# Four of eight experts on 64 slots, with both parts of the tokens side by side

## The chip, the core and the metric

The kernel runs on one core of a Trainium2 chip. A core has TensorE (PE in the profile; its weight loads are shown apart, as PEld), VectorE (DVE), ScalarE (ACT), GpSimd (POOL) and SyncE (SP), which have instruction queues of their own and wait for one another through semaphores. Here SP issues nearly all DMA transfers. The metric is the device time of one execution, in microseconds (us), as the median of several runs.

## What is computed

Two layers of a decoder trunk on 256 tokens of width 1024, in float32. Each layer is a mixer, a cross attention to 256 memory tokens and a feed-forward part. The feed-forward part is dense in the first layer and a mixture of eight experts in the second. Only the mixture matters here; its hidden width is 2816 (11 x 256).

```python
def swiglu(h, w_gate, w_up, w_down):
    a = jnp.einsum("bsd,df->bsf", h, w_gate)
    u = jnp.einsum("bsd,df->bsf", h, w_up)
    return jnp.einsum("bsf,fd->bsd", jax.nn.silu(a) * u, w_down)

def moe_swiglu(h, router_w, w_gate, w_up, w_down):
    logits = jnp.einsum("bsd,de->bse", h, router_w).astype(jnp.float32)
    top_v, top_i = lax.top_k(logits, TOP_K)          # TOP_K = 2, N_EXPERTS = 8
    top_w = jax.nn.softmax(top_v, axis=-1)
    gates = jnp.sum(jax.nn.one_hot(top_i, N_EXPERTS) * top_w[..., None], axis=-2)
    y = jnp.zeros(h.shape, jnp.float32)
    for e in range(N_EXPERTS):
        y = y + gates[..., e:e + 1] * swiglu(h, w_gate[e], w_up[e], w_down[e])
    return y
```

256 tokens choose two experts each, so the eight lists hold 512 entries, 64 on average. The reference's router, evaluated on the reference's inputs, gives the experts 0 to 7 lists of 61, 68, 51, 64, 63, 68, 68 and 69 tokens.

## The kernel before

**Products in three passes.** A float32 product is made of float32r products: both operands are split into a part `h` (high) and a rest `l` (low), and `mm3` (L325 to L328) adds low times high, high times low and high times high. So a tile of the weights passes through TensorE three times: its high part twice (L326 with the tokens' low part as stationary operand, L328 with their high part), its low part once (L327).

**Weights.** All weights come in tiles of [128, 2048] float32 (1 MiB, 1.049 MB). `weight_order` lists them in the order of their use. `load` (L134) issues a tile's DMA on SP into a free stage buffer; a buffer is free again when its tile has been split. In the mixture there are eleven stage buffers: four in the pool `wst`, four in `wst2` and three that `spare` takes elsewhere (`wsp` in the rows). `halve` splits a tile: for each half of 1024 columns ACT writes the high part `wh` (L143), then DVE writes the rest `wl` in two pieces of `CUT` = 512 columns (L147). The halves lie in rings of `HALVES` = 5 tiles [128, 1024] each for `wh` and `wl`, that is, two and a half weight tiles. `w` hands out the next tile and sees to it that the tiles up to two behind it (`split_ahead`) are split.

**The mixture (`moe`).** The router's choice is made on the chip: `route` gives `pos`, the place of each token in each expert's list (from 1; 0 where the expert isn't taken), and `pp`, whose last eight columns are the lengths of the lists. `prepare` and `gather` fetch the tokens of two experts at a time: one-hot matrices `oh` [tokens, 128 slots] times the tokens give each expert its 128 slots, feature-major (`xg`), again as a high and a low part. Every expert has 128 slots, whatever its list's length. An expert has 11 chunks (256 hidden columns each). A chunk takes two tiles `gu` (gate and up side by side, 2 x 4 blocks of 128 features) and one tile `dn`:

- `eg`: 8 blocks x 3 passes of 512 columns (24 matmuls) on the expert's tokens give [128 slots, gate 256 | up 256];
- `es`: ACT takes the silu of the gates (L1141), DVE multiplies it by the ups (L1142);
- `turn`: PE transposes `es` (2 transposes, L1087), ACT and DVE split the result into `ehh` and `ehl` (L336, L340);
- `down`: 2 x 2 x 3 = 12 matmuls add to `ed` [128 slots, 1024].

At an expert's end `evacuate` splits `ed` into `yh` and `yl`, and `scatter` brings the rows back to the tokens (`ez`, 8 matmuls) and adds them, times the gates, to the residual stream `x` (L1128). These steps overlap: the transposes belong to the chunk before, `down` to the one before that. Each engine's instructions run in the order in which the Tile scheduler placed them.

The experts run in the order 0 to 7. Behind the last one a register holds the longest list's length (`longest`); where it is over 128, a loop goes over all eight experts again for the slots from 128 on.

**Where it stands in time.** In the profile the mixer, the cross attention and the dense part of both layers take the first 580 us, the router 580 to 598 us, and the eight experts 598 to 1390 us.

Of the kernel before, what the change touches and what calls it, by code (L numbers as in the profile page):

```python
# [7 lines left out]
F32 = mybir.dt.float32  # L8
# [8 lines left out]
P = 128  # L17
# [40 lines left out]
class Halves:  # L58
    """A weight tile [128, 2048] as two tiles of its columns, each freed on its own."""
# [10 lines left out]
class Trunk:  # L70
    """The whole network as one Tile program; the residual stream stays in SBUF.

    A float32 product is three passes of float32r: both operands are split exactly into a
    part of float32r's precision and the rest, and only rest * rest (below float32's last
    bit) is left out.
    """

    def __init__(self, ctx, tc, a, out):
# [5 lines left out]
        self.split_ahead = 1  # L84
        self.build()

# [1 line left out]
    def weight_order(self):  # L88
# [3 lines left out]
        for l in range(DEPTH):  # L92
# [21 lines left out]
            else:  # L114
                m = l // 2
                gu = [(("gu", l, e * NFC + fc, k), a["moe_gu"][m, e, fc, k])
                      for e in range(E) for fc in range(NFC) for k in range(2)]
                dn = [(("dn", l, e * NFC + fc), rows(a["moe_w_down"][m, e], fc)) for e in range(E) for fc in range(NFC)]
# [9 lines left out]

    def load(self, src):
        """A weight tile into a free stage buffer."""  # L130
        slot = self.free.pop(0)
        st = slot()
        dst = st.rearrange("p (a b) -> p a b", b=src.shape[2]) if len(src.shape) == 3 else st
        self.fetched = self.nc.sync.dma_start(dst, src)  # L134
        return slot, st

    def halve(self, slot, st):
        """hi + lo = a staged tile; its buffer is free again."""
        nc, tc = self.nc, self.tc
        wh, wl = [Halves(*[self.wp.tile([P, 1024], F32R, name=n) for _ in range(2)]) for n in ("wh", "wl")]  # L140
        for q in range(2):
            s = slice(q * 1024, (q + 1) * 1024)
            self.halved = nc.scalar.activation(wh[:, s], st[:, s], AF.Copy)  # L143
            for c in range(0, 1024, CUT):
                s = slice(q * 1024 + c, q * 1024 + c + CUT)
# [5 lines left out]
    def spare(self):  # L151
        """One more stage buffer."""
# [19 lines left out]
    def w(self, *key):  # L172
        """The next weight tile, as two float32r parts [128, 2048]."""
# [6 lines left out]
    def build(self):  # L180
# [20 lines left out]
        with tc.tile_pool(name="mid", bufs=1) as self.md, tc.tile_pool(name="wkb", bufs=2) as self.wb:  # L201
            with tc.tile_pool(name="tmp", bufs=1) as tmp:
# [8 lines left out]
                # NEG where the column is beyond the row, and where it is before it  # L211
# [10 lines left out]
                # sel[p, h] is one where p is h or 32 + h  # L222
# [10 lines left out]
                # slot numbers along the row (from 1), and e' < e  # L233
# [31 lines left out]
        with tc.tile_pool(name="emid", bufs=1) as self.md, tc.tile_pool(name="ewkb", bufs=2) as self.wb, \  # L265
# [3 lines left out]
            self.xg = [self.big("xg", shape=(P, 2 * KD * P)) for _ in range(3)]  # L269
# [3 lines left out]
    def warm(self, n):  # L273
        """Keeps the tensor engine's clock up where it would wait."""
# [1066 lines left out]
```

## Time and profile before

| what | value |
|---|---|
| median of 3 runs | 1406.48 us (1405.11 to 1407.85) |
| the profiled execution, span from the first to the last instruction | 1404.0 us |
| PE busy | 1376.4 us (98%) |
| PEld busy | 1156.1 us (82%) |
| DVE busy | 1218.4 us (87%) |
| ACT busy | 946.2 us (67%) |
| moved by DMA | 368.09 MB, mean 262 GB/s |

The median is 2.5 us over the profiled execution's span; sums below are made against the span. The profile's page gives the busy time of each engine, then 40 equal slices of the span with the busy share of each engine in tenths, then the DMA queues, the chain of work that ended last, and the costliest groups of instructions. An instruction's duration runs from its start to the end of its last write, and the next one on the same engine may start before that end; so what an instruction costs its engine is the distance to the next start, and this is read from the timeline.

### The profile page before, as it was taken

The page shows a single profiled execution, that of the slowest core. Times are in us where ns is not written, and L with a number is a line of the kernel's source. Part 1 is how long each engine was busy: PE and PEld are TensorE (multiplying, and loading weights), DVE is VectorE, ACT ScalarE, POOL GpSimd, SP SyncE. Part 2 cuts the span into 40 slices and gives each one's busy share as a digit, 9 for nine tenths or more (in the row PEclk, how much of TensorE's full clock was granted, in tenths as well). Part 3 has the DMA queues.
Part 4 walks back from the last instruction along what each step waited for, and adds up shares of the span by engine and source line. Part 5 has one row for each costly group of instructions (what it writes and reads, how often), then busy time and mean ns, then how long its engine had stood idle before and what let it go on. Part 6 is the DMA issues. An engine that isn't in the chain of part 4 may idle for free.

```text
span 1404.0 us, 21087 instructions
## 1 busy us (share of the span) xinstructions
PE 1376.4 (98%) x7489; PEld 1156.1 (82%) x7489; DVE 1218.4 (87%) x2556; ACT 946.2 (67%) x1457; POOL 8.1 (1%) x30
## 2 busy tenths in 40 slices
PE   9999999999999999799999999999999999999996
PEld 9878989999998778688888888888788888888884
DVE  7988876655688887799999999899999999999997
ACT  7565575444455646587877877777777777777774
POOL 0000000000000000000000000000000000000000
PEclk9999999999999999899999999999999999999998
DMA  8422635555454224779988999889999989999870
GB/s 311 172 73 118 210 105 204 194 189 180 180 188 157 83 91 179 280 297 364 367 338 333 362 344 366 334 318 346 357 354 364 353 318 353 350 363 366 317 273 33
DMA packets 67569, 368.09 MB, mean 262 GB/s; under 512 B 5744, under 2 KB 6000, under 8 KB 38016
## 3 DMA queue, kind: packets, MB, share of 16 engines
q1 hardware_dynamic: 67136, 365.59, 69.7%
q8 instruction: 61, 1.00, 0.3%
q0 software_dynamic: 320, 1.08, 0.2%
q14 instruction: 52, 0.43, 0.1%
HBM read 365.60 MB, written 1.05 MB: 261 GB/s over the span
## 4 chain that ended last, share of the span: by engine, by line
PE 90%; DVE 5%; ACT 2%; DMA 2%; issue 1%; DVEq 0%; ACTq 0%; SPq 0%; POOL 0%; POOLq 0%
PE eg L327 11%; PE eg L326 11%; PE eg L328 11%; PE fm L327 6%; PE fm L326 6%; PE fm L328 6%; PE ed L326 5%; PE ed L328 5%; PE ed L327 5%; DVE wl L147 3%; PE tm L327 2%; PE tm L328 2%; PE tm L326 2%; PE pr L326 1%; PE pr L327 1%; PE pr L328 1%
## 5 line engine op out<-in xcount | busy, mean ns | idle before, releaser
L147 DVE TENSOR_TENSOR wl<-wst,wh 128x512 fp32r<-128x512 f32 x1100 | 694.6, 685 | 106.0 <-ACT wh L143 103.6
L143 ACT ACTIVATE wh<-wst 128x1024 fp32r<-128x1024 f32 x550 | 562.1, 1058 | 183.3 <-PE fm L328 90.9
L327 PE MATMUL eg<-wl,xg 128*128 128x512 f32 x704 | 282.4, 401 | 0.1
L326 PE MATMUL eg<-wh,xg 128*128 128x512 f32 x704 | 278.9, 396 | 0.0
L328 PE MATMUL eg<-wh,xg 128*128 128x512 f32 x704 | 278.1, 395 | 0.0
L326 PE MATMUL fm<-hTh,wl 128*128 128x256 f32 x736 | 206.8, 281 | 0.3 <-DVE wl L147 0.3
L327 PE MATMUL fm<-hTl,wh 128*128 128x256 f32 x736 | 206.2, 280 | 0.0
L328 PE MATMUL fm<-hTh,wh 128*128 128x256 f32 x736 | 205.6, 279 | 0.0
L147 DVE TENSOR_TENSOR wl<-wsp,wh 128x512 fp32r<-128x512 f32 x280 | 175.5, 686 | 11.0 <-ACT wh L143 10.0
L326 PEld LDWEIGHTS eg<-wh,xg 128*128 128x128 f32 x704 | 132.3, 188 | 31.0
L327 PEld LDWEIGHTS eg<-wl,xg 128*128 128x128 f32 x704 | 132.3, 188 | 30.2 <-DVE wl L147 1.2
L328 PEld LDWEIGHTS eg<-wh,xg 128*128 128x128 f32 x704 | 132.4, 188 | 29.4
L143 ACT ACTIVATE wh<-wsp 128x1024 fp32r<-128x1024 f32 x140 | 142.4, 1055 | 13.9 <-ACT wh L143 7.0
L326 PEld LDWEIGHTS fm<-hTh,wl 128*128 128x128 f32 x736 | 138.4, 188 | 1.1 <-DVE wl L147 0.4
L327 PE MATMUL ed<-wl,ehh 128*128 128x512 f32 x352 | 139.2, 395 | 0.0
L328 PE MATMUL ed<-wh,ehh 128*128 128x512 f32 x352 | 139.1, 395 | 0.0
L327 PEld LDWEIGHTS fm<-hTl,wh 128*128 128x128 f32 x736 | 138.4, 188 | 0.9 <-issue 0.2
L328 PEld LDWEIGHTS fm<-hTh,wh 128*128 128x128 f32 x736 | 138.4, 188 | 0.0
L326 PE MATMUL ed<-wh,ehl 128*128 128x512 f32 x352 | 133.4, 405 | 0.0
L1141 ACT ACTIVATE es<-eg,xr 128x256 f32<-128x256 f32 x88 | 41.9, 477 | 71.5 <-PE eg L328 71.5
L328 PEld LDWEIGHTS ed<-wh,ehh 128*128 128x128 f32 x352 | 66.0, 188 | 15.7
L327 PEld LDWEIGHTS ed<-wl,ehh 128*128 128x128 f32 x352 | 66.1, 188 | 14.2
(297 smaller groups left out, 1702.8 us busy)
## 6 DMA issues: line engine op xcount, KB each, us to landing
wst<-in_moe_gu_dram SPq DMA_DIRECT2D x130, 1024.0 KB, 5.0
wst<-in_moe_w_down_dram SPq DMA_DIRECT2D x64, 1024.0 KB, 5.0
wsp<-in_moe_gu_dram SPq DMA_DIRECT2D x46, 1024.0 KB, 5.0
wsp<-in_moe_w_down_dram SPq DMA_DIRECT2D x24, 1024.0 KB, 5.0
wst<-in_ffn_gu_dram SPq DMA_DIRECT2D x22, 1024.0 KB, 4.8
wst<-in_w_in_fm_dram SPq DMA_DIRECT2D x16, 1024.0 KB, 5.0
wst<-in_ffn_w_down_dram SPq DMA_DIRECT2D x11, 1024.0 KB, 4.8
wst<-in_w_in_tm_dram SPq DMA_DIRECT2D x8, 1024.0 KB, 5.0
```

Source lines behind the costliest of these rows:

```text
L143: self.halved = nc.scalar.activation(wh[:, s], st[:, s], AF.Copy)
L147: nc.vector.tensor_tensor(wl[:, s], st[:, s], wh[:, s].bitcast(F32), op=ALU.subtract)
L326: nc.tensor.matmul(out, ll, rh, start=start, stop=False)
L327: nc.tensor.matmul(out, lh, rl, start=False, stop=False)
L328: nc.tensor.matmul(out, lh, rh, start=False, stop=stop)
L1141: nc.scalar.activation(s, pg[:, 0:256], AF.Silu, scale=xr)
```

## The change

1. **Order of the experts.** `sort` (new, called in `moe` behind the gates) ranks the lists of experts 0 to 6 by length on DVE and writes the experts' numbers in that order to `ids`; SP loads these seven numbers into registers. Expert 7 stays first (place 0), since its weights are loaded before the router has run. The places 1, 3, 5 and 7 get the four shortest of the seven lists, the places 2, 4 and 6 the three longest. The weights of the places 1 to 7 are loaded from addresses that depend on these registers (`expert_gu`, `expert_dn`). `pos` and `gates` are brought into the same order.
2. **Short experts.** The places 1, 3, 5 and 7 run `short`: 64 slots. The stationary operand of a pass is [128 features, 64 slots high | 64 slots low], so each of `wl` and `wh` passes once; the rows 0 to 63 of the result belong to the high part, the rows 64 to 127 to the low one. ACT copies the result from PSUM (`eg`); `turn` is now four products of `eg` with `comb`, a [128, 64] matrix that adds both parts, times 1 / rms; then ACT's silu, DVE's product and the split. `ehh` holds both parts side by side too, and `down` has 8 matmuls for 12.
3. **Gather.** The groups are (0), (1, 2), (3, 4), (5, 6), (7) instead of pairs. A short list's one-hot columns are written twice, and its gather takes 64 columns.
4. **Splits of 1024 columns.** From the mixture on DVE writes `wl` in one piece for each half (`CUT[1]` = 1024).
5. **Buffers.** `wst2` has three buffers instead of four, `xg` two big tiles instead of three, and the freed tile is one more `spare`: again eleven stage buffers.
6. **The loop behind the end** runs where a list of the places 1, 3, 5, 7 is over 64, or another over 128; it then goes over all eight experts.

`evacuate` and `scatter` are moved out of `expert` with the same content. The core of the diff:

```diff
-CUT = 512
-STAGES = (4, 4)
+CUT = (512, 1024)
+STAGES = (4, 3)
+C = 64
+NSHORT = 4
+PLACES = (None, 0, 4, 1, 5, 2, 6, 3)
+GROUPS = ((0,), (1, 2), (3, 4), (5, 6), (7,))
...
+    def expert_gu(self, m, q, fc, hf):
+        gu = self.a["moe_gu"]
+        if q == 0:
+            return gu[m, E - 1, fc, hf]
+        return lambda: gu[m, bass.ds(self.ids[PLACES[q]], 1), fc, hf].rearrange("o p n -> p (o n)")
...
-            for c in range(0, 1024, CUT):
-                s = slice(q * 1024 + c, q * 1024 + c + CUT)
+            for c in range(0, 1024, self.cut):
+                s = slice(q * 1024 + c, q * 1024 + c + self.cut)
...
-            self.xg = [self.big("xg", shape=(P, 2 * KD * P)) for _ in range(3)]
+            self.xg = [self.big("xg", shape=(P, 2 * KD * P)) for _ in range(2)]
+            self.spare()
...
+    def sort(self, pos, gates, pp):
+        nc, md = self.nc, self.md
+        F = E - 1
+        cnt = md.tile([P, E], F32, name="cnt")
+        nc.vector.tensor_copy(cnt, pp[:, 2 * E:3 * E])
...
+        nc.vector.tensor_tensor(g2, oth, own, op=ALU.is_equal)
+        nc.vector.tensor_tensor(g1, oth, own, op=ALU.is_lt)
...
+        nc.vector.tensor_scalar(ids, num[:, 0], -1.0, None, op0=ALU.add)
...
+        self.ids = [nc.values_load(ids[0:1, r:r + 1], engines=[mybir.EngineType.SP], min_val=0, max_val=F - 1)
+                    for r in range(F)]
...
+        def short(gu, dn, x, xr, oh, gate, at):
...
+            both = x.rearrange("p k s t -> p k (s t)")
+            comb = wb.tile([P, C], F32, name="comb")
+            nc.vector.tensor_scalar(comb, eye, xr, None, op0=ALU.mult)
+            def turn(fc, g):
+                pt = self.psum((P, 4, C), "et")
+                for b in range(4):
+                    nc.tensor.matmul(pt[:, b, :], g[:, b * P:(b + 1) * P], comb, start=True, stop=True)
+                s = wb.tile([P, 256], F32, name="es")[:, 0:2 * C].rearrange("p (k t) -> p k t", t=C)
+                nc.scalar.activation(s, pt[:, 0:2, :], AF.Silu)
+                nc.vector.tensor_tensor(s, s, pt[:, 2:4, :], op=ALU.mult)
+                h = wb.tile([P, 2, P], F32R, name="ehh", bufs=3).rearrange("p k (s t) -> p k s t", t=C)
+                self.split(h[:, :, 0, :], h[:, :, 1, :], s)
+                later(lambda: down(fc, h))
+            def down(fc, h):
+                wh, wl = dn(fc)
+                for n in range(2):
+                    for k in range(2):
+                        fs = slice(k * 1024 + n * 512, k * 1024 + (n + 1) * 512)
+                        for w in (wl, wh):
+                            nc.tensor.matmul(ps[n], h[:, k].rearrange("p s t -> p (s t)"), w[:, fs], start=fc == 0 and k == 0 and w is wl,
...
+                        for w in (wl, wh):
+                            nc.tensor.matmul(pg, both[:, c], w[:, fs], start=c == 0 and w is wl,
+                                             stop=c == KD - 1 and w is wh)
+                g = wb.tile([P, 512], F32, name="eg", bufs=1)
+                nc.scalar.activation(g, pg, AF.Copy)
...
+                if q % 2:
+                    short(gu, dn, xg[m], xr[:, m:m + 1], oh[:, :, m, :], gate, at)
+                else:
+                    expert(gu, dn, xg[m], xr[:, m:m + 1], oh[:, :, m, :], gate, at, first if q == 0 else ())
```

How this moves instructions, at three places. In these rows an instruction stands as line, operation, out<-in and shape; a number behind a name is the buffer's.

PE, in the second expert, two blocks of a chunk's `eg`, of the kernel before:

```order
L326 MATMUL eg_8130<-wh_8041,xg_6686 128x512
L327 MATMUL eg_8130<-wl_8043,xg_6686 128x512
L328 MATMUL eg_8130<-wh_8041,xg_6686 128x512
L326 MATMUL eg_8130<-wh_8074,xg_6686 128x512
L327 MATMUL eg_8130<-wl_8076,xg_6686 128x512
L328 MATMUL eg_8130<-wh_8074,xg_6686 128x512
```

and of the changed kernel, in the first short expert, with the products of the chunk before (L1246) behind the first tile's blocks:

```order
L1273 MATMUL eg_8081<-wl_8027,xs_6693 128x512
L1273 MATMUL eg_8081<-wh_8025,xs_6693 128x512
L1246 MATMUL et_8120<-comb_7854,eg_8042 128x64 x3
L1273 MATMUL eg_8081<-wl_8057,xs_6693 128x512
L1273 MATMUL eg_8081<-wh_8055,xs_6693 128x512
```

Two passes stand where three stood, with `xs` (both parts of the tokens) as the one stationary operand.

DVE, in the same stretch, one chunk (three tiles) of the kernel before:

```order
L1142 SCALAR_TENSOR_TENSOR es<-eg,xr_10065,es 128x256
L147 TENSOR_TENSOR wl<-wst,wh 128x512 x4
L340 TENSOR_TENSOR ehl<-et,ehh 128x256
L147 TENSOR_TENSOR wl<-wst,wh 128x512 x8
L1142 SCALAR_TENSOR_TENSOR es<-eg,xr_10065,es 128x256
```

and of the changed kernel in a short expert:

```order
L1249 TENSOR_TENSOR es<-es,et 128x128
L169 TENSOR_TENSOR wl<-wst,wh 128x1024 x2
L363 TENSOR_TENSOR ehh<-es,ehh 128x2x64
L169 TENSOR_TENSOR wl<-wsp,wh 128x1024 x4
L1249 TENSOR_TENSOR es<-es,et 128x128
```

Twelve splits became six of twice the width, and the two other instructions have half the columns. The product L1249 waits for ACT's silu, the split L363 for ACT's half of the same split.

ACT, in the same stretch, one chunk of the changed kernel:

```order
L1276 ACTIVATE eg<-eg 128x512
L359 ACTIVATE ehh<-es 128x2x64
L165 ACTIVATE wh<-wst 128x1024 x4
L1248 ACTIVATE es<-et 128x128
L165 ACTIVATE wh<-wst 128x1024 x2
```

of the kernel before:

```order
L1141 ACTIVATE es<-eg,xr_10065 128x256
L143 ACTIVATE wh<-wst 128x1024 x2
L336 ACTIVATE ehh<-et 128x256
L143 ACTIVATE wh<-wst 128x1024 x4
```

The copy of `eg` is new, and the silu stands behind four of the chunk's six splits.

## Rows read from the trace of the kernel before

**Rows 1.** The page: GB/s in 40 slices of the span, main queue, largest DMA issues.

```profile
GB/s 311 172 73 118 210 105 204 194 189 180 180 188 157 83 91 179 280 297 364 367 338 333 362 344 366 334 318 346 357 354 364 353 318 353 350 363 366 317 273 33
...
q1 hardware_dynamic: 67136, 365.59, 69.7%
...
wst<-in_moe_gu_dram SPq DMA_DIRECT2D x130, 1024.0 KB, 5.0
```

**Rows 2.** Windows: PE, PEld, DVE, ACT, POOL busy (x instructions), PEclk, DMA share, GB/s.

```profile
700.00:750.00 50.00, 50.00 (x234) 40.84 (x233) 49.30 (x93) 40.23 (x56) 0.00 (x0) 1.00 0.89 337
1250.00:1300.00 50.00, 50.00 (x223) 40.27 (x222) 47.24 (x83) 38.27 (x47) 0.00 (x0) 1.00 0.97 367
```

**Rows 3.** The instructions of tile `eg`: duration min/median/max, first and last start.

```profile
L326 PE MATMUL eg<-wh,xg x704: 389/395/486, 598.4 to 1378.5; 128*128 128x512 f32 x176
```

**Rows 4.** Timeline: start, us, engine, instruction; runs of equal ones are merged.

```profile
583.91 1.12 DVE L342 SCALAR_TENSOR_TENSOR hTl<-hnt,prm,hTh 128x128 fp32r<-128x128 f32 x4
...
1374.34 3.89 ACT L143 ACTIVATE wh<-wst 128x1024 fp32r<-128x1024 f32 x4
...
1375.43 4.91 DVE L147 TENSOR_TENSOR wl<-wst,wh 128x512 fp32r<-128x512 f32 x8 [0.18 <-ACT wh L143]
...
1376.19 0.40 PE L328 MATMUL eg<-wh,xg 128*128 128x512 f32 x1
...
1376.89 0.40 PE L328 MATMUL eg<-wh,xg 128*128 128x512 f32 x1
```

**Rows 5.** Groups, 600 to 1380 us: shapes, count | busy us, mean ns | idle before.

```profile
L147 DVE TENSOR_TENSOR wl<-wst,wh 128x512 fp32r<-128x512 f32 x758 | 471.7, 685 | 20.0 <-ACT wh L143 18.1
...
L340 DVE TENSOR_TENSOR ehl<-et,ehh 128x256 fp32r<-128x256 f32 x87 | 36.1, 415 | 0.2 <-ACT ehh L336 0.2
...
L1128 DVE SCALAR_TENSOR_TENSOR x<-ez,gates,x 128x512 f32<-128x512 f32 x28 | 20.1, 741 | 0.0
```

**Rows 6.** Waits, 620 to 1360 us: who for whom, total us, times, longest.

```profile
ACT es L1141 <- PE eg L328: 69.4, 82, 3.1
ACT ehh L336 <- PE et L1087: 47.7, 41, 2.7
DVE wl L147 <- ACT wh L143: 24.9, 72, 1.2
...
SPq L134 <- DVE wl L147: 640.7, 245, 5.3
```

**Rows 7.** Timeline in the mixer: float32 products of 65 columns, each two passes.

```profile
118.80 0.39 PE L741 MATMUL mh<-v,ws 128*128 128x65 f32 x2
119.02 0.39 PE L742 MATMUL mh<-v,ws 128*128 128x65 f32 x2
```

**Rows 8.** Timeline of DVE between the router's steps.

```profile
590.42 0.15 DVE L355 TENSOR_TENSOR rs_t<-rs_t,rs_v 128x2 f32<-128x2 f32 x1
590.49 0.16 DVE L1169 TENSOR_REDUCE emax<-lg 128x2 f32<-128x16 f32 x1
```

**Rows 9.** SP's register load ahead of the experts: duration, first and last start.

```profile
L1203 SPq TENSOR_LOAD <-mxi x1: 465/465/465, 593.2 to 593.2; - x1
```

**Rows 10.** Timeline of SP: first and last of 13 loads for the experts, the next.

```profile
542.30 22.80 SPq L134 DMA_DIRECT2D wst<-in_moe_gu_dram  x4
...
594.15 0.38 SPq L134 DMA_DIRECT2D wsp<-in_moe_w_down_dram  x1
602.83 0.33 SPq L134 DMA_DIRECT2D wst<-in_moe_gu_dram  x1
```

**Rows 11.** Windows of 5 and 10 us, with the columns of rows 2.

```profile
565.00:570.00 5.00, 3.60 (x15) 2.81 (x16) 2.38 (x5) 2.37 (x5) 0.00 (x0) 1.00 0.80 306
570.00:575.00 5.00, 5.00 (x24) 4.08 (x23) 0.48 (x2) 0.91 (x2) 0.00 (x0) 1.00 1.02 424
...
650.00:655.00 5.00, 5.00 (x24) 4.05 (x23) 4.57 (x10) 4.05 (x6) 0.00 (x0) 1.00 0.99 412
...
1360.00:1370.00 10.00, 10.00 (x50) 8.22 (x49) 8.90 (x17) 7.86 (x11) 0.00 (x0) 1.00 0.01 4
```

More of the change, by code (lines that the diff above doesn't have):

```diff
@@ L1021, in moe @@
         norm = self.norm
+        twice = md.tile([P, 2, C], BF16, name="twice")
+        eye = md.tile([P, C], F32, name="eye")
+        xs = md.tile([P, 2 * KD * C], F32R, name="xs")
         def halves(i, n):
@@ L1034, in moe, with gather @@
         self.split_ahead = 2
+        self.cut = CUT[1]
         rms = norm.keep.tile([P, NT], F32, name="ncol")
[L1037 to L1041 removed]
+        def gather(lists, xg):
+            oh = lists[0][0]
+            lo = C if lists[0][1] else 0
+            w = len(lists) * P - lo
+            ohs = oh.rearrange("p i n s -> p i (n s)")
+            xg = [t.rearrange("p (k s t) -> p k s t", s=2, t=C) if short else t.rearrange("p (s k t) -> p k s t", s=2, t=P)
+                  for t, (_, short) in zip(xg, lists)]
+            xr = wb.tile([P, len(lists)], F32, name=f"xr{len(lists)}")
             def steps():
@@ L1057, in steps @@
                 ps = self.psum(name="xr")
-                for m in range(n):
+                for m in range(len(lists)):
                     for i in range(NT):
@@ L1078, in drain, with later, evacuate, scatter @@
                 behind()
-        def expert(gu, dn, xh, xl, xr, oh, gate, at=lambda fc: None, pre=()):
+        def later(step):
+            downs.append(step)
+            if len(downs) == 1:
+                downs.insert(0, lambda: None)
+        def evacuate(ps, oh, gate):
+            y = []
+            po = self.psum(name="eo")
+            for i in range(NT):
+                nc.tensor.transpose(po[:, i * P:(i + 1) * P], oh[:, i, :].bitcast(F32), self.ident)
+            oT = wb.tile([P, T], F32R, name="oT", bufs=1)
+            nc.vector.tensor_copy(oT, po[:, 0:T])
+            for n in range(2):
+                yh = wb.tile([P, 512], F32R, name="yh")
+                yl = wb.tile([P, 512], F32R, name="yl")
+                self.split(yh, yl, ps[n])
+                y.append((yh, yl))
+            adds.append(lambda: None)
+            for i in range(NT):
+                adds.append(lambda i=i: scatter(i, oT, y, gate))
+        def scatter(i, oT, y, gate):
+            ts = slice(i * P, (i + 1) * P)
+            for n in range(2):
+                pz = self.psum(name="ez")
+                nc.tensor.matmul(pz, oT[:, ts], y[n][1], start=True, stop=False)
+                nc.tensor.matmul(pz, oT[:, ts], y[n][0], start=False, stop=True)
+                xs = self.x[:, i, n * 512:(n + 1) * 512]
+                nc.vector.scalar_tensor_tensor(xs, pz, gate(i), xs, op0=ALU.mult, op1=ALU.add)
+        def expert(gu, dn, x, xr, oh, gate, at=lambda fc: None, pre=()):
             ps = [self.psum(name="ed") for _ in range(2)]
@@ new lines, in moe, with prepare @@
+        groups = {}
+        lists = (pos, None)
+        def prepare(n):
+            places = GROUPS[n]
+            oh = wb.tile([P, NT, len(places), P], F32R, name="oh")
+            which = [(oh, q % 2 == 1) for q in places]
+            for i in range(NT):
+                for m, q in enumerate(places):
+                    p = pos[:, i, E - 1:E] if q == 0 else by[0][:, i, PLACES[q]:PLACES[q] + 1]
+                    src = twice.rearrange("p s t -> p (s t)") if which[m][1] else self.slots
+                    at = nc.vector.tensor_scalar(oh[:, i, m, :], src, p, None, op0=ALU.is_equal)
+            if n == 0:
@@ L1157, in prepare @@
                 self.hold = at
-            xg, xr, steps = gather(oh, NP, [self.xg[(p * NP + n) % 3] for n in range(NP)])
-            pairs[p] = oh, xg, xr
+            xg, xr, steps = gather(which, [self.xg[q // 2 % 2] if q % 2 == 0 else xs for q in places])
+            groups[n] = oh, xg, xr
             return steps
```

162 lines of the change are left out of this document (92 added, 70 removed).

## The prediction

> **What bounds the kernel now.** I began with the page. PE is busy for 98% of the span, DVE for 87% (the table above). The GB/s line [rows 1] falls into two parts: up to about 580 us the core moves 73 to 311 GB/s, and from there, in the experts, 273 to 367. The experts are the part that the change touches, so their windows are the next view. There PE is busy for 50.00 of 50 us, DVE for 47.24 and 49.30, ACT for 38 to 40 [rows 2]. DVE is no bound yet, but it is 3% short of one.
>
> How long an expert takes is read from the first and the last `eg`: 598.4 to 1378.5 us for eight [rows 3], **97.5 us each**. What an instruction costs its engine is read from the starts in the timeline: three passes of 512 columns, from one L328 to the next, take 0.70 us, 0.233 us each; eight DVE splits of 512 columns take 4.91 us, the last of them 0.685 us, so 0.604 us each [rows 4, 5]. An expert has 11 x (24 + 12) = 396 passes, 92.3 us; the other 5.2 us of PE are transposes, gather and scatter. DVE has 33 x 4 = 132 splits, 79.7 us; its busy share in the windows, 0.965, makes 94.1 us for an expert, so 14.4 us are other work.
>
> The queue of the weights is ahead: SP waits 640.7 us in all for DVE to free a buffer [rows 6]. So the transfers follow the engines today and set nothing.
>
> **Short experts.** *Passes.* Each loses a third: 264 passes, 61.5 us, 30.8 us less. New are four float32 products in a chunk. The nearest rows have 65 columns: one starts 0.22 us behind the other and shows as two passes [rows 7]; 44 of them make 9.7 us. With scatter PE needs about **74 us**; the transposes are gone, and a short list's gather runs in the long expert before it.
>
> *Splits.* They are not fewer: the weights are split as before, 33 tiles. But a piece has 1024 columns. The trace has no such split. Between 256 and 512 columns the duration grows from 415 to 685 ns [rows 5], so 512 more columns cost 0.540 us: 1.144 us a piece. The ends are 1.08 (no fixed part at all) and 1.21 (twice today's). 66 pieces are 75.5 us, 4.2 less than now.
>
> *The rest of DVE.* `es` and `ehh`, 22 instructions of 128 columns: four such take 1.12 us [rows 4], at most 0.28 each, 6 us. Four additions to `x` at no more than 0.741 us [rows 5], 3 us; `yl`, `oT` and small ones 1.5 us. Sum: **86 us**. So in a short expert DVE is the bound, and PE waits for it.
>
> *ACT.* 66 high parts at 0.97 us [rows 4] are 64 us; the copy of `eg` (at most 0.97 us for half those columns, so about 0.5), the silu and `ehh` make some 12 us more. 76 us lie beside DVE's 86.
>
> *What joins the engines.* `wh` and `wl` have rings of two and a half tiles. DVE has time to spare in a long expert, so it enters a short one up to two tiles ahead; two tiles of 2.6 us are 5 us that PE needn't wait, and DVE wins them back in the next long expert. Against that stand DVE's waits for ACT, 24.9 us in the stage now, 3 us an expert [rows 6]. Net 2 us: I take **84 us** for a short expert, with 80 (the lead counts in full) and 92 (no lead, waits of 6 us) as ends.
>
> **Long experts.** PE has the same 396 passes. DVE needs 75.5 + 14.4 us and its gather, 91 to 92 us: still covered by PE, so the wider splits give nothing here. The gather of both lists of a group now stands in the long expert, where it was spread over two: 16 more matmuls than the average, each with 192 columns for 256. A pass costs between 0.11 us (65 columns, [rows 7]) and 0.233 us, and the narrower ones give some back: 0 to 2.5 us. I take 1.2 and count **98.7 us**.
>
> **Start and end.** `sort` puts about 28 small instructions on DVE between the router and the first splits, and SP waits for them; two of today's small ones there start 0.07 us apart [rows 8]; at 0.1 us each, since many of the new ones are wider, this is 3 us. The first group has one list instead of two: 8 of 16 gather splits of 128 columns fewer, 2 us. Together +1 us, with -2 and +4 as ends. On SP seven register loads stand behind each other, 0.465 us each [rows 9], with their checks under 6 us. Behind them is a load of weights that now goes out at 594.15; the one after it waits until 602.83 for its buffer anyway [rows 10], and a tile is used ten tiles later. So this is hidden by the buffers; without that cover it would cost its 6 us once. The address arithmetic of each load adds an instruction to SP, which is idle for most of 2.6 us between two loads. The end is one short chunk's chain instead of a long one's: I count 0.
>
> **Transfers.** This is the cover that gets thin. Of the experts' 264 tiles (8 x 33, two of three of them like the row of `gu` in [rows 1]) 13 are issued before 602.83 [rows 10]; 251 tiles, 263 MB, remain, and from 1360, 44 us before the end, hardly anything moves [rows 11]. Today they take 757 us, 347 GB/s. In my forecast they get 709 us (1356 less 603 and 44), 371 GB/s. While its packets moved, the queue did 365.59 MB in 69.7% of 1404 us, 374 GB/s [rows 1]. In single windows it did 424 and, among the experts, 412 [rows 11]. So the transfers just fit, with the lower of these rates as the nearest rival bound: 263 MB at 374 GB/s is 703 us, an end at 1350, below the forecast.
>
> **The sum.** Eight experts now: 780.1 us. Then: 4 x 98.7 + 4 x 84 = 730.8. Difference -49.3, start +1. From the span of 1404.0 this leaves 1355.7; with the 2.5 us by which the median is above the span, **1358 us**.
>
> **Rivals.** *DVE waits in every chunk (slower).* In a short chunk the work goes from PE to ACT (copy), PE (products), ACT (silu), DVE (product), ACT and DVE (split), and all queues are in order. ACT takes such waits today at no cost: 69.4 us in 82 times for `eg`, 47.7 us in 41 times for the transposes, 0.85 and 1.16 us each [rows 6]. If DVE, now the bound, took both in each chunk, a short expert would be 86 + 22 = 108 us, the eight 827, the time 1454. It decides from 10 us an expert, 0.9 us a chunk: there a pair is as long as today's. For it: three engines within 12 us of each other and rings of five halves. Against it: DVE's order has two to four splits between the steps of that chain, and PE and DVE run at 1.00 and 0.965 now without PE waiting. Chance 0.08; a part of it, with times of 1374 to 1400, 0.07.
>
> *The transfers become the bound.* If what the slices of the experts show, 354 GB/s in their middle [rows 1], is not what was asked for but what the memory gives over long stretches, 263 MB take 743 us, the end is 603 + 743 + 44 = 1390 and the time 1392. For it: the 40 slices never exceed 367 once the experts run, and the 424 lasted for 5 us. Against it: SP's waits are for buffers, and 50 us went at 367 [rows 2]. Chance 0.06. The page "DMA: Bandwidth & Descriptors" of the Trainium skill (the table at its top) gives such a limit, a core's share of the HBM bandwidth, of about 358 GB/s; by it the transfers would need 735 us and the time would be 1385. The trace does not agree: 367 over 50 us and 424 over 5 us are above it.
>
> *Nothing to gain:* DVE at 1.21 us a piece and waits of 6 us make a short expert 97 us, and the time stays: 0.02.
>
> *The lists don't fit.* The fourth shortest of the seven lists has exactly 64 tokens. One more in it, and the loop goes over eight experts again: eight times 97.5 us more, about 2140 us. The reference's lists fit, and the closest second and third choices there are 0.004 apart, at logits of up to 17. Chance 0.02.
>
> *PE's clock.* A PE that waits may be granted less. It would work for 74 of 84 us; in the stretch with 3.60 of 5 us busy the clock was still 1.00 [rows 11]. I count nothing.
>
> **How the numbers follow.** The forecast and what lies within 1340 to 1373 has 0.75; transfers 0.06; partial waits 0.07; no change 0.02; slower by DVE's waits 0.08; lists 0.02. The range takes in the ends of the short expert (80 us: 1342; 92 us: 1390, about the transfers' 1392): 1340 to 1390. Faster by over 0.2% (about what a measurement of this kernel can tell from no change) has 0.75 + 0.06 + 0.07 = 0.88, the same 0.02, slower 0.10.
>
> **What would show it.** A split of 1024 columns near 1.23 us in duration and 1.14 between starts. In the windows, an alternation: about 98 us with PE at 50 of 50, then about 84 us with DVE at 49 or more and PE near 44. SP still waiting for buffers. Wrong would be: `wh` waiting for a DMA for many us (transfers), DVE below 46 of 50 in the short experts (the chain), or a PEclk below 1.00 there.

## The result, and the profile after

The changed kernel takes **1389.59 us** (median of 4 runs, 1387.14 to 1390.80) where the kernel before takes 1406.35 us on the same chip: a ratio of 0.988, with a 95% interval of 0.987 to 0.990. That is 16.8 us less, where 48 were forecast. The profiled execution has a span of 1388.5 us.

Where the time went is read by experts. An expert starts at its first `eg`; in us, from the starts in the two traces (the first and the last start of before are those in [rows 3]):

| place | before | after | forecast |
|---|---|---|---|
| start of the first | 598.4 | 603.7 | +1 |
| 0, long | 89.7 | 95.8 | 98.7 |
| 1, short | 101.5 | 83.5 | 84 |
| 2, long | 96.7 | 106.3 | 98.7 |
| 3, short | 101.5 | 88.8 | 84 |
| 4, long | 97.2 | 102.5 | 98.7 |
| 5, short | 101.5 | 90.7 | 84 |
| 6, long | 96.9 | 102.7 | 98.7 |
| 7, short | 95.1 | 88.9 | 84 |
| last `eg` to the end | 25.5 | 25.6 | +0 |

One lone matmul of place 2 stands at 778.9 us, among the last of place 1; there, and wherever one stands so in the kernels below, a place is counted from its second matmul (783.0).

Windows over the places 1, 2, 3 and 5 of the changed kernel; in a row stand the length, the busy time of PE, PEld, DVE, ACT and POOL with their instructions, then the granted clock, the DMA engines' share and GB/s:

```profile
700.00:783.00 83.00, 80.97 (x372) 60.25 (x370) 82.08 (x91) 76.96 (x101) 0.00 (x0) 1.00 0.99 390
783.00:889.00 106.00, 101.56 (x459) 81.66 (x458) 96.70 (x122) 79.07 (x108) 0.00 (x0) 0.98 0.91 340
...
889.00:978.00 89.00, 80.93 (x366) 60.07 (x366) 83.81 (x97) 73.26 (x100) 0.00 (x0) 1.00 0.98 381
...
1081.00:1171.00 90.00, 80.66 (x363) 59.14 (x362) 83.34 (x94) 72.20 (x99) 0.00 (x0) 1.00 0.98 372
```

The first short expert has the length and the bound that were forecast: DVE is busy for 82.08 of 83 us. In the others DVE idles for 5 to 7 us and PE for 8 or 9, so neither is full, though each short expert has the same work. The waits at place 5 (engine, tile, line, what it waited for: us in all, times, the longest) say who waits:

```profile
ACT es L1248 <- PE et L1246: 15.1, 10, 2.2
...
DVE wl L169 <- ACT wh L165: 4.9, 8, 0.7
```

One chunk of such an expert on ACT and on DVE, from the timeline at place 7 (start, us, engine, line, operation, tiles, count, and in brackets the idle time ahead with its releaser):

```profile
1329.58 0.59 ACT L1276 ACTIVATE eg<-eg 128x512 f32<-128x512 f32 x1
1330.06 0.31 ACT L359 ACTIVATE ehh<-es 128x128 fp32r<-128x128 f32 x1
1330.26 3.90 ACT L165 ACTIVATE wh<-wst 128x1024 fp32r<-128x1024 f32 x4
1335.69 0.28 ACT L1248 ACTIVATE es<-et 128x128 f32<-128x128 f32 x1 [1.53 <-PE et L1246]
1335.86 2.00 ACT L165 ACTIVATE wh<-wst 128x1024 fp32r<-128x1024 f32 x2
1337.76 0.59 ACT L1276 ACTIVATE eg<-eg 128x512 f32<-128x512 f32 x1
```

```profile
1331.35 4.63 DVE L169 TENSOR_TENSOR wl<-wst,wh 128x1024 fp32r<-128x1024 f32 x4
1336.00 0.29 DVE L1249 TENSOR_TENSOR es<-es,et 128x128 f32<-128x128 f32 x1
1336.95 2.36 DVE L169 TENSOR_TENSOR wl<-wst,wh 128x1024 fp32r<-128x1024 f32 x2 [0.66 <-ACT wh L165]
```

ACT has made four halves and stands at the silu, which waits 1.53 us for PE's `et`. The next high part begins only behind it, at 1335.86. DVE finishes the four halves at 1336.0, then the product that the silu released, and then has nothing for 0.66 us. From copy to copy the chunk takes 8.18 us.

The pieces themselves cost what was read from before. The row of the wide splits (busy, mean ns) has 1221 ns, against 685 for a narrow one in [rows 5]:

```profile
L169 DVE TENSOR_TENSOR wl<-wsp,wh 128x1024 fp32r<-128x1024 f32 x188 | 222.7, 1221 | 18.8 <-ACT wh L165 16.7
```

At place 2, the longest, PE stands still once for 4.2 us. Its first matmul of the next group's gather waits for `oh`. On DVE the first of the four `oh` stands behind splits and the additions of place 1's scatter, and the other three behind two splits more:

```profile
PE xg L1132 <- DVE oh L1292: 4.2, 1, 4.2
```

```profile
819.19 0.74 DVE L1192 SCALAR_TENSOR_TENSOR x<-ez,sorted,x 128x512 f32<-128x512 f32 x1
819.85 0.28 DVE L1292 TENSOR_SCALAR oh<-twice,sorted 128x128 fp32r<-128x128 bf16 x1
820.04 2.35 DVE L169 TENSOR_TENSOR wl<-wsp,wh 128x1024 fp32r<-128x1024 f32 x2
822.31 0.28 DVE L1292 TENSOR_SCALAR oh<-slots,sorted 128x128 fp32r<-128x128 bf16 x1
```

### The profile page after: what moved, and what is told of

The parts are those of the page before. It is cut to its first block, busy times and chain, and to the rows that moved or that the text cites. A ratio compares the mean times of both kernels' runs of the same rounds, so it can differ in the third digit from the quotient of the medians.

```text
span 1388.5 us, 20513 instructions
## 1 busy us (share of the span) xinstructions
PE 1324.8 (95%) x7257; PEld 1090.6 (79%) x7257; DVE 1175.7 (85%) x2059; ACT 949.5 (68%) x1501; POOL 8.1 (1%) x30
## 4 chain that ended last, share of the span: by engine, by line
PE 71%; DVE 12%; DMA 10%; ACT 4%; issue 3%; DVEq 0%; SPq 0%; ACTq 0%
DVE wl L169 9%; PE fm L349 6%; PE fm L351 6%; PE fm L350 6%; PE eg L1273 6%; PE eg L350 5%; PE eg L349 5%; PE eg L351 5%; DMA wst<-in_moe_gu_dram 4%; DMA wst<-in_moe_w_down_dram 2%; ACT wh L165 2%; PE ed L349 2%; PE ed L351 2%; PE ed L350 2%; PE ed L1260 2%
## 5 line engine op out<-in xcount | busy, mean ns | idle before, releaser
L169 DVE TENSOR_TENSOR wl<-wst,wh 128x512 fp32r<-128x512 f32 (+1 forms) x668 | 614.0, 955 | 116.2 <-ACT wh L165 113.8
L169 DVE TENSOR_TENSOR wl<-wsp,wh 128x1024 fp32r<-128x1024 f32 x188 | 222.7, 1221 | 18.8 <-ACT wh L165 16.7
L1273 PE MATMUL eg<-wl,xs 128*128 128x512 f32 x352 | 149.2, 424 | 12.2 <-DVE wl L169 11.6
L350 PE MATMUL eg<-wl,xg 128*128 128x512 f32 x352 | 141.9, 403 | 2.8 <-DVE wl L169 2.6
L349 PE MATMUL eg<-wh,xg 128*128 128x512 f32 x352 | 141.6, 402 | 0.0
L351 PE MATMUL eg<-wh,xg 128*128 128x512 f32 x352 | 140.0, 398 | 0.0
L1273 PE MATMUL eg<-wh,xs 128*128 128x512 f32 x352 | 138.4, 393 | 0.0
L1273 PEld LDWEIGHTS eg<-wl,xs 128*128 128x128 f32 x352 | 66.3, 188 | 41.5 <-DVE wl L169 19.0
L350 PEld LDWEIGHTS eg<-wl,xg 128*128 128x128 f32 x352 | 66.9, 190 | 21.2 <-DVE wl L169 6.9
L349 PEld LDWEIGHTS eg<-wh,xg 128*128 128x128 f32 x352 | 67.0, 190 | 15.9 <-ACT wh L165 0.8
L351 PEld LDWEIGHTS eg<-wh,xg 128*128 128x128 f32 x352 | 66.7, 189 | 15.3
L1273 PEld LDWEIGHTS eg<-wh,xs 128*128 128x128 f32 x352 | 66.5, 189 | 10.0
```

Of the source, the lines that this page charges most:

```text
L169: nc.vector.tensor_tensor(wl[:, s], st[:, s], wh[:, s].bitcast(F32), op=ALU.subtract)
L349: nc.tensor.matmul(out, ll, rh, start=start, stop=False)
L350: nc.tensor.matmul(out, lh, rl, start=False, stop=False)
L351: nc.tensor.matmul(out, lh, rh, start=False, stop=stop)
L1273: nc.tensor.matmul(pg, both[:, c], w[:, fs], start=c == 0 and w is wl, stop=c == KD - 1 and w is wh)
```

## The experiments

All ratios to the kernel before are of runs on the same chip; the chips of the rounds differ, and the kernel before has medians of 1404.7 to 1406.4 us on them. Times are medians; each kernel has its own profile, and the table is of that one execution. Two theories stand against each other in the expectations: A, the order of ACT's queue, in which an instruction that waits for PE holds up the high parts behind it; B, the transfers. The short and long experts by place, in us:

| kernel | start | 0 | 1 short | 2 | 3 short | 4 | 5 short | 6 | 7 short |
|---|---|---|---|---|---|---|---|---|---|
| after | 603.7 | 95.8 | 83.5 | 106.3 | 88.8 | 102.5 | 90.7 | 102.7 | 88.9 |
| narrow splits | 608.3 | 95.2 | 90.1 | 108.1 | 88.2 | 101.9 | 87.5 | 101.4 | 87.3 |
| half the bytes | 599.7 | 95.6 | 83.5 | 105.2 | 83.5 | 106.4 | 83.5 | 104.3 | 87.0 |
| silu a chunk later | 600.6 | 93.2 | 83.4 | 100.5 | 89.1 | 102.5 | 88.8 | 102.6 | 88.7 |
| silu behind one more half | 600.9 | 96.2 | 83.5 | 106.4 | 86.6 | 102.5 | 88.5 | 102.7 | 87.7 |
| copy behind both tiles | 601.4 | 95.5 | 83.5 | 107.7 | 87.7 | 102.7 | 89.6 | 102.9 | 87.8 |
| order of place 1 | 603.8 | 95.8 | 83.5 | 106.3 | 82.9 | 102.0 | 84.3 | 102.2 | 83.5 |
| `oh` early | 600.5 | 96.1 | 83.5 | 100.3 | 91.0 | 102.5 | 90.7 | 102.7 | 89.0 |
| silu behind one more half, `oh` early | 600.8 | 95.6 | 83.5 | 100.3 | 88.5 | 102.5 | 88.5 | 102.7 | 87.7 |
| the same, narrow in long ones | 602.2 | 96.0 | 83.5 | 101.1 | 88.5 | 101.9 | 88.5 | 101.4 | 88.7 |
| order, `oh` early | 600.6 | 95.2 | 83.5 | 100.3 | 84.7 | 102.0 | 84.3 | 102.2 | 83.5 |
| order, `oh` early, narrow splits | 602.5 | 95.9 | 90.0 | 101.7 | 86.8 | 101.9 | 87.3 | 101.4 | 87.2 |

**Wide splits alone, in the kernel before.**

```diff
-            for c in range(0, 1024, CUT):
+            for c in range(0, 1024, CUT if self.split_ahead == 1 else 1024):
```

> The kernel before, with pieces of 1024 columns for the wl splits of the mixture and nothing else. The first two theories of why the changed kernel is 31 us slower than forecast (A: in a short expert ACT's queue has the silu, which waits for et from PE, ahead of the next wh, and DVE waits 0.66 us a chunk for that; B: transfers) say nothing of it. Since PE is busy for 98% of the span of before, the relief of DVE (about 4 us an expert) should be hidden: 1406 us, within 3. Against this stands that DVE, with more room, could remove small waits of PE (up to 8 us in all, 1398), or that PE waits longer for the first columns of a tile (0.5 us later in each half; 1410 or more).

Measured: 1413.09 us, ratio 1.005 (1.004 to 1.007), 7.8 us more than the 1405.28 of before. Experts 3 to 7 are 0.8 to 1.6 us longer each. The relief of DVE bought nothing, as said, and the wider hand-over cost, the second of the two objections. In the waits from 890 us on, of before

```profile
PEld eg L327 <- DVE wl L147: 1.2, 4, 0.5
```

became, with wide pieces,

```profile
PEld eg L327 <- DVE wl L147: 12.4, 34, 0.6
```

**Narrow splits in the changed kernel.**

```diff
-CUT = (512, 1024)
+CUT = (512, 512)
```

> The changed kernel with the wl splits in pieces of 512 columns again. DVE then has 132 pieces of 0.604 us instead of 66 of 1.14, 4.2 us more an expert. Theory A (DVE stands in a loop of three engines in the short experts, so each of its instructions counts there): +17 us by four short experts, 1407; up to 1415 if the long experts, where DVE is busy 96 of 103 us, are touched too. Theory B (the transfers set the short experts): no change, 1390.

Measured: 1392.78 us, 3 us more than the changed kernel, far below theory A's 1407 and near theory B's 1390. (The table's row is of an execution of 1396.9 us; it begins late because the granted clock is 0.54 in the window from 508 to 523 us.) By the table only the first short expert pays, 6.6 us. The other three are 0.6 to 3.2 us *shorter* with 4 us more work on DVE. So in them DVE's work is not the length, and the simple form of theory A, in which each of its instructions counts, is wrong.

**Half the bytes.** Only half of each weight tile of the mixture is loaded, and both halves of the split read it:

```diff
+        if part:
+            src = src[:, 0:1] if len(src.shape) == 3 else src[:, 0:1024]
...
+            return slot, Twice(st)
```

> The changed kernel with half of each weight tile of the mixture loaded (512 KB for 1 MB; both halves of the tile are split from the half that is there, so the numbers of the experts are not the model's and all work on the engines stays). Theory B (the DMA engines' busy share is 0.98 in the short experts and a landing takes 7.0 us for 5.0 before): the time falls by 15 us or more, towards 1358 to 1375. Theory A, and any theory in which the engines set the time: 1387 to 1391, no change, since a tile lies in its buffer for 13 us or more before ACT starts on it.

Measured: 1376.96 us, 12.6 us less, 2 us short of the range that the transfers' theory gave. But the table shows more: the places 3 and 5 have exactly the 83.5 us of place 1, which place 1 had with full transfers too. The instructions stand in another order: this edit of the loads was enough to change what the scheduler made of the rest of the code. In the changed kernel ACT has two orders. At place 1, and with half the bytes at the other short places, a chunk is

```
L1276 eg<-eg | L165 wh x4 | L359 ehh<-es | L165 wh | L1248 es<-et | L165 wh
```

and at the places 3, 5 and 7

```
L1276 eg<-eg | L359 ehh<-es | L165 wh x4 | L1248 es<-et | L165 wh x2
```

Counted by weight tiles, the copy `eg` (L1276) of a chunk stands in the first behind four halves beyond the tiles that it needs itself, in the second behind two; the silu comes five halves later in the first, four in the second. So the run did not tell transfers and order apart; later ones do.

**Silu, product and split a chunk later.**

```diff
+                silus.append(lambda: silu(fc, pt))
+
+            def silu(fc, pt):
...
-            lead = 3 if l % 2 == 0 else 6
+            lead = 3 if l % 2 == 0 else 8
```

> The changed kernel with turn of the short experts cut in two: the four products run where they ran, but silu, product and split of that chunk come one chunk later, and down of all experts one chunk later. ACT then finds et done. Theory A: the waits of the silu for et (1.5 to 1.8 us a chunk) go, a chunk takes DVE's 7.45 us instead of 8.15, a short expert about 83 to 86 instead of 89 to 91 (the first short one, 83.5 now, keeps its time), the end costs up to 2 us: 1371 to 1381. Theory B, and a theory C in which DVE's own work and not its waits is the length of a short expert: 1388 to 1392.

Measured: 1379.61 us, in the expected range and for another reason. The short experts at 3 and 7 are as long as before, since the scheduler put the silu ahead of the same splits and ACT still waits 1.47 us a chunk for `et`. The gain lies in the long experts at 0 (2.6 us) and 2 (5.8 us) and ahead of the mixture (3.1 us); the end is 1.7 us longer. It says nothing for theory A.

**One half more ahead of the silu.**

```diff
+                with tc.issue_after(self.firsts[0].ins):
                     nc.scalar.activation(s, pt[:, 0:2, :], AF.Silu)
```

> The changed kernel with one thing fixed: in a short expert the silu is issued on ACT behind the first half of one weight tile more. Theory A2 (the order on ACT, and not a queue of transfers, makes the short experts at the places 3, 5 and 7 last 88 to 91 us; the first short expert, which the scheduler placed in another order, lasts 83.5 us): all short experts at 83 to 85 us, 17 us less; as with the halved transfers, the next long expert then begins with DVE behind and loses 2 to 4 us, twice: 1376 to 1382. Theory B2 (the halved transfers gained their 13 us because fewer bytes moved): the full transfers are back, 1388 to 1392.

Measured: 1383.85 us, ratio 0.985 (0.983 to 0.987). That lies between the ranges of the two theories. Short experts lose 1.2 to 2.2 us, not 5 to 7. In the trace the silu came further back than intended, behind the next chunk's copy and so six halves behind its own, while the copy has two halves beyond its tiles as before. At place 5 the wait has moved from the silu to the copy, and DVE's is nearly what it was:

```profile
ACT eg L1280 <- PE eg L1277: 16.7, 11, 2.7
...
DVE wl L172 <- ACT wh L166: 4.5, 8, 0.6
```

**The one-hot matrices a chunk earlier** (the gather where it was).

```diff
-                    if m == len(places) - 1 and fc == 3 and n + 1 < len(GROUPS):
+                    if m == len(places) - 1 and fc == 2 and n + 1 < len(GROUPS):
                         steps = prepare(n + 1)
-                    next(steps, None)
+                    else:
+                        next(steps, None)
```

> The changed kernel with the one-hot matrices of the next group made one chunk earlier (fc = 2 instead of 3) and its gather where it was. Theory: in the long expert at place 2 PE waits 4.2 us for oh, which stands on DVE behind splits that are late, and the clock falls for 3.4 us: 4 to 6 us less, 1384 to 1386. Rival: DVE is behind there whatever the order is, and PE then waits 4 us for wl instead: 1389 to 1391.

Measured: 1384.99 us, as expected. Place 2 takes 100.3 us for 106.3, and no wait for `wl` takes the place of the one that went. Place 3 gives 2.2 us back; another 3.2 us between the two profiled executions are the start, which this edit does not explain (below).

**Both of these.**

> Both of the two edits. If both theories hold: short experts 83 to 85, long ones 102 to 103 without the 4 us at their first chunks: 1366 to 1372. If only the order on ACT counts: 1376 to 1382. If neither: 1388 to 1392.

Measured: 1379.25 us (ratio 0.982, 0.980 to 0.984): place 2 as in the second, the short experts as in the first; the theory of the silu alone falls here as well. The time lies in the range for "only the order on ACT counts", but by luck: place 2 gained 6.0 us by `oh`, and the short experts kept 87.7 to 88.5 us.

**Both, with narrow splits in long experts.**

```diff
         def expert(gu, dn, x, xr, oh, gate, at=lambda fc: None, pre=()):
...
+            self.cut = CUT[0]
...
         def short(gu, dn, x, xr, oh, gate, at):
...
+            self.cut = CUT[1]
```

> The two edits, and splits of 512 columns while a long expert runs, of 1024 while a short one does. The kernel before lost 7 us with the wide splits in long experts alone (1 to 1.6 us in each from the fourth on), and the changed kernel's long experts at the places 4 and 6 are 0.6 and 1.3 us shorter with narrow ones. If that holds here, 3 to 5 us less than with the two edits alone. Rival: DVE, with 4.2 us more work in a long expert, enters the short ones without a lead: 2 to 8 us more than with the two edits alone.

Measured: 1379.05 us, no difference to the run before it. The long experts at 4 and 6 are 0.6 and 1.3 us shorter, the long one at 2 and the short one at 7 0.8 and 1.0 us longer, and the start is 1.4 us later, where the granted clock of this execution is 0.72 in the window from 569 to 575 us.

**The order of the first short expert in all four.** The copy is issued behind the last half of the newest tile, and the silu behind the first half of the newest tile, ahead of the second. In the trace the copy has four halves beyond its tiles and the silu comes five halves later, as at place 1 (`ehh` stands three halves earlier than there):

```diff
+                with tc.issue_after(self.newest.ins), self.urgent():
                     nc.scalar.activation(s, pt[:, 0:2, :], AF.Silu)
...
+                with tc.issue_after(self.halved.ins):
                     nc.scalar.activation(g, pg, AF.Copy)
```

> The changed kernel with two places fixed on ACT in the short experts: the copy of eg stands behind the halves of both tiles that follow the two it needs (in the short experts at the places 3, 5 and 7 the scheduler put it behind one of them, in the first behind both), and the silu three halves behind the copy instead of four halves behind it counted from the earlier place. That is the first short expert's order for all four. Theory A3 (ACT must have four halves ready for DVE when it comes to an instruction that waits for PE; with two, DVE runs dry 0.66 us a chunk, and moving the silu alone only moved this wait to the copy): short experts at the places 3, 5, 7 at 83 to 85 us instead of 88.8, 90.7 and 88.9, the long ones behind them 0 to 4 us longer because DVE comes in late: 1372 to 1380. Theory B2 (the halved transfers gained by fewer bytes, and 98% busy DMA engines set these experts): 88 to 91 us stay, 1384 to 1391.

Measured: **1370.32 us**, ratio 0.974 (0.973 to 0.976), with the full transfers. Places 3, 5 and 7 take 82.9, 84.3 and 83.5 us; up to place 3 the trace is that of the changed kernel to 0.1 us. The total is 2 us below theory A3's range, because the long experts behind short ones are 0.5 us shorter and not 0 to 4 longer. At place 3 DVE is busy for 82.41 of 83 us:

```profile
889.00:972.00 83.00, 81.21 (x366) 59.65 (x365) 82.41 (x95) 72.97 (x99) 0.00 (x0) 1.00 0.99 389
```

A chunk at place 7, on ACT:

```profile
1315.08 0.58 ACT L1280 ACTIVATE eg<-eg 128x512 f32<-128x512 f32 x1
1315.56 1.05 ACT L165 ACTIVATE wh<-wst 128x1024 fp32r<-128x1024 f32 x1
1317.26 0.31 ACT L361 ACTIVATE ehh<-es 128x128 fp32r<-128x128 f32 x1 [0.65 <-DVE es L1252]
1317.47 2.94 ACT L165 ACTIVATE wh<-wst 128x1024 fp32r<-128x1024 f32 x3
...
1321.27 0.26 ACT L1251 ACTIVATE es<-et 128x128 f32<-128x128 f32 x1
...
1322.37 0.58 ACT L1280 ACTIVATE eg<-eg 128x512 f32<-128x512 f32 x1
```

Neither the copy nor the silu waits for PE any more; ACT's one wait is for DVE, which has no idle time left to lose. From copy to copy the chunk takes 7.29 us for 8.18 (7.29 is the median at the places 3 and 5 too, where the changed kernel has 8.17, and 7.41 at place 1), and DVE's waits for `wh` in the whole expert are

```profile
DVE wl L171 <- ACT wh L165: 0.5, 1, 0.5
```

**The copy alone.**

```diff
+                with tc.issue_after(self.halved.ins):
                     nc.scalar.activation(g, pg, AF.Copy)
```

> Only the copy of eg is fixed behind the halves of both tiles, the silu where the scheduler then puts it (two halves behind the copy, and a quick test for et). Theory A3: the copy no longer waits, the silu does (PE needs two weight tiles' time from the copy to et): 85 to 88 us a short expert, 1378 to 1385. Theory B2: 1384 to 1391.

Measured: 1388.02 us, above theory A3's range and inside theory B2's, which the run before it has ruled out. The silu, now two halves behind the copy, takes the wait over, and DVE waits as before (place 5):

```profile
ACT es L1248 <- PE et L1246: 15.3, 10, 2.9
...
DVE wl L169 <- ACT wh L165: 4.3, 7, 0.7
```

So it takes both. With two halves ahead of the copy and four between it and the silu the places 3, 5 and 7 take 88.8 to 90.7 us, with two and six 86.6 to 88.5, with four and two 87.7 to 89.6, with four and five 82.9 to 84.3. Nothing between these was run.

**The order, and the one-hot matrices early.**

> The order of the first of these three runs, and the one-hot matrices one chunk earlier, which took 6 us from the long expert at place 2. If both hold: short 83 to 85, long 100 to 104: 1364 to 1372. If DVE's lateness after a fast short expert shows up as waits for wl in the long one: 1372 to 1378.

Measured: **1364.72 us**, ratio 0.971 (0.969 to 0.973), some 25 us less than the changed kernel and faster than both kernels. The short experts sum to 336.0 us, four times the 84 of the forecast.

**The same with narrow splits.**

> The fastest kernel so far (the order of the first short expert in all four, one-hot matrices one chunk earlier) with the wl splits in pieces of 512 columns again. If DVE's own work is now what a short expert lasts, and the wider pieces save it 4.2 us an expert as the starts in the trace say: each short expert 4 us or more longer, 1381 or more, while with the scheduler's order the same edit cost 3 us in all because DVE's waits took it in. If DVE is still not the bound there: 1363 to 1370.

Measured: 1383.91 us, 19.2 us more. The short experts are 6.5, 2.1, 3.0 and 3.7 us longer (4 or more were expected of each); where DVE is the bound, its pieces' width counts, and where it waits for ACT anyway it does not (3 us in the scheduler's order).

## Why the prediction was half right

The direction, the price of each instruction and the bound of a short expert were right; the time was 32.8 us too low (1355.7 for a span of 1388.5). By the table:

**Short experts: 15.9 us of it.** The forecast of 84 us each is a sum: 75.5 us for 66 splits, 10.5 us for DVE's other work, less a lead of 5 us, and 3 us of waits for ACT. DVE as the bound and the price of a split hold (1221 ns long, four in 4.63 us). The lead and the waits failed. Of the instructions that touch `wl` (busy time of PE, PEld and DVE, then the clock, the DMA engines' share and GB/s), place 3 in the changed kernel and with the mended order:

```profile
889.30:978.05 88.75, 56.08 (x132) 24.62 (x131) 74.65 (x65) 1.00 0.98 380
```

```profile
889.40:972.30 82.90, 56.76 (x132) 24.62 (x131) 74.74 (x66) 1.00 0.99 389
```

A lead of 5 us would have left 70.5 us of splits inside the place. 74.65 us are there, so the lead was 0.9 us at most. The waits, taken from the kernel before at 3 us an expert, are 4.9, 4.9 and 5.2 us at the places 3, 5 and 7. The remaining 9.2 us of place 3 are a little less than the 10.5 for other work. With the mended order the splits are the same, the wait is 0.5 us, and the place takes 82.9: so it is ACT's order that makes these experts long. That all four then sum to 336.0 us, four times 84, is luck in part, since a lead of 0.8 us for 5, waits of 0.5 to 1.0 us for 3 and other work of 8 to 9 us for 10.5 about cancel.

This was the rival "DVE waits in every chunk", in its partial form with times of 1374 to 1400. The argument against it, that two to four splits stand between the steps of the chain, holds for DVE's order. On ACT the places of the copy and of the silu decide, and the copy has only two halves ready beyond it. The order of ACT's chunk that stands ahead of the prediction is this one, and it was read without counting those halves.

The measured time lies just inside the range, 1340 to 1390, whose upper end was worked out for short experts of 92 us. They took 88.0 us on average; the rest of the way came from the long experts and the start, which the range left as counted. So that it lies inside is luck in part as well.

**Long experts: 12.5 us.** 3.7 us are a misreading. The 97.5 us are a mean of long experts with and without a gather, and of a first one of 89.7 us. The gather of a pair stood in every second expert, where PE had 32 matmuls more; of the instructions that touch `xg` (PE, PEld, DVE, ACT), in the windows over the places 5 and 6 of before:

```profile
1085.00:1186.50 101.50, 69.22 (x296) 53.21 (x296) 4.56 (x16) 4.57 (x16) 1.00 0.92 342
1186.50:1283.40 96.90, 65.72 (x265) 48.77 (x264) 0.00 (x0) 0.00 (x0) 1.00 0.95 358
```

So a gather costs about 4.5 us (101.5 less 97), all of it now in each long expert, and 1.2 was too little; by rows of before the four would have been 94.2, 101.2, 101.7 and 101.4. Of the remaining 8.8 us 5.1 are place 2, with its wait for `oh`: made one chunk earlier, `oh` costs no wait and the place takes 100.3. It is the place of `oh` in DVE's queue and not a DVE that comes late out of a short expert: with the mended order the long experts at 4 and 6 follow short ones that DVE fills, and take 102.0 and 102.2 us, no more than before the order was mended. At 4 and 6, 0.8 and 1.3 us are the wide split: with narrow ones the two take 101.9 and 101.4, and it costs a long expert 0.8 to 1.6 us in the kernel before as well; "the wider splits give nothing here" should have been "cost a little". The rest, 1.6 us, is the first expert, which begins at the lower clock (below). Its length follows how long that lasts: 95.2 us where the lower level goes on for 2.9 us behind the first `eg` (order, `oh` early), 95.8 for 4.1 us (the changed kernel), 96.2 for 4.9 us (silu behind one more half).

**Start: 4.3 us.** The step that was counted came out. PE's matmuls just ahead of the router, at 575 to 585 us of before, are 4.4 us late in the changed kernel, and its first `eg` is 5.3 us late: the router with `sort` adds 0.9 us, where +1 was forecast. What failed is that nothing was counted ahead of the router. The profiled execution of the changed kernel has two short falls of the granted clock there, and they cost 3.2 us (by 1.6 us more the same matmuls are late behind each). The other 1.2 us come without a fall too: in the kernels with full loads whose clock did not fall ahead of the mixture the same matmuls are 1.2 to 2.0 us late, and the first `eg`, at 600.5 to 601.4, 0.9 to 1.0 us more. Where these come from stays open. Window 569 to 575 us of before, then of the changed kernel:

```profile
569.00:575.00 6.00, 6.00 (x28) 4.90 (x27) 0.91 (x3) 1.20 (x3) 0.00 (x0) 1.00 1.01 422
```

```profile
569.00:575.00 6.00, 5.03 (x16) 3.83 (x15) 2.38 (x5) 1.16 (x4) 0.00 (x0) 0.72 0.95 397
```

**End:** 0, as counted (25.6 us for 25.5).

**The transfers** were no bound, as forecast: with full loads and the mended order the core moved 389 GB/s through a short expert of 83 us, and the order alone gave 19 us; with half the bytes (201 GB/s) and the order of place 1 an expert takes the same 83.5 us. The rival of 354 GB/s falls with this; that its time, 1392, was close to the measured one is chance. The limit of about 358 GB/s on the page "DMA: Bandwidth & Descriptors" of the Trainium skill (the table at its top) does not hold here. The page "Perfetto Trace Analysis" of the Trainium skill (section "Roofline") calls that figure a share for two active cores and lets a single core draw more, up to some 120% of it. The trace agrees with that, at 109%.

**PE's clock** was counted at nothing. In the short experts that is right: 1.00 with PE busy for 81 of 89 us. At place 2 the clock fell behind PE's stop of 4.2 us, and the window there shows 0.98. The start has the larger cost, 3.2 us.

## What to carry to other kernels

When three engines with queues in order share a loop, the sum of each engine's work gives the length only if an engine that must wait has handed over enough work ahead of the wait. A lead that one engine is to bring along belongs into such a sum only once it has been counted in pieces. Count, for each instruction that waits for a slower engine, how many pieces stand ahead of it beyond those that the wait itself needs, and do so at every place, since a scheduler may order the same code in two ways. Moving one waiting instruction moved the wait to the next one here, twice; and a cheaper load, or any edit that changes what the scheduler believes, can change the order, and the change can pass for an effect of its own.

## What was not expected of the hardware

- The core's transfers reached 389 GB/s over 83 us with the DMA engines' share at 0.99, and in the changed kernel landings took 7.0 us (median) for 5.0 before; from 600 to 1364 us its engines waited for them three times, 1.5 us in all.
- PE's busy time hides small waits. In the kernel before with wide splits PE is busy for 498 of 499 us, and yet the experts are 1 us longer; the row of PEld, 12.4 us of waits for `wl`, shows it.
- At the router the granted clock stayed at 0.53 on average from 590 to 608 us, where before it was 0.72 from 586 to 604 with PE about equally busy (13.3 and 13.0 us of 18). The first chunk of the first expert ran at the lower level for it. What decides the length of that stretch, and the two falls ahead of the mixture, stays open; of the kernels made from the changed one three more have a fall at 569 or 570 us (0.72 in the same window), the one with narrow splits has one of 0.54 from 508 to 523 us, and the others have none.
